# Attention values of a hybrid encoder: one stage for all heads, tokens stationary and weights moving

## The chip, the core and the metric

The kernel runs on one core of a Trainium2 chip. The time is the device time of one launch in microseconds (us) (the span in the profile is the part of it from the first to the last recorded instruction); lower is better. Engines are named TensorE (PE in the profile, PEld for its weight loads), VectorE (DVE), ScalarE (ACT), GpSimd (POOL) and SyncE (SP, which here issues DMAs).

## What is computed

One layer of a streaming encoder for 512 prompt tokens and 64 tokens of a later chunk that share the weights. A combined projection is split among three head groups (a gated delta rule, differential attention, pooling), whose outputs are mixed, and a feed-forward part follows. The change is about `bv`, the values of the attention:

```python
h = rmsnorm(x, norm_mix)                       # (512 + 64) x 1024
proj = jnp.einsum('bld,de->ble', h, w_in)
aq, ak, av, az, aa, ab, bq, bk, bv, cx = split_cols(proj, IN_WIDTHS)
...                                            # A: gated delta rule over aq, ak, av, gate az
bv4 = bv.reshape(bsz, length, B_HEADS, B_DV)   # 4 heads of 128
w = diff_softmax_weights(s, lam)               # softmax_1 - lam * softmax_2
o_b = jnp.einsum('bhqk,bkhe->bqhe', w, bv4)    # later chunk: with 512 cached keys and values ahead
new_v = bv4                                    # an output: p_v, s_v
...                                            # C: pooling over cx
x = x + jnp.einsum('ble,ed->bld', jnp.concatenate([o_a, o_b, o_c], -1), w_out)
x = x + conv_ffn(rmsnorm(x, norm_ffn), ...)
```

## The kernel before

**Tiling.** All 576 tokens stay in SBUF with the features on the partitions. A gemm makes 128 output features for all tokens: the weight tile is stationary, 576 tokens move past it in two parts of 256 and 320 columns (`PARTS`). Each operand is split into a rounded fp32r part and the fp32r remainder (`w_hi` by a ScalarE cast, line 174; `w_lo` by a VectorE subtraction, line 175), and a product is hi x hi + hi x lo + lo x hi. So one gemm (`gemm`, matmuls recorded at line 85) is 8 k tiles x 3 products x 2 parts = 48 matmuls into one accumulator of two PSUM banks (`psg`, named `g`; two such tiles rotate). Four more PSUM banks (`psm`, named `m`) serve everything small.

**Order.** TensorE's instructions are issued in the order in which the program writes them. `projections` is the main stream; it yields after each matmul group, and `drive` then lets the generators that are due (`spawn`) write their own steps in between, by a clock that counts an estimate of TensorE time. A generator that waits for a flag (`after`) makes the stream skip ahead to the next due one, so that no gemm stands between.

**Stages.** `projections` makes, head by head, k, q and v of the delta rule, each followed by a `front(h)` (transposes at line 89, squares, scaling evictions at line 630, then five score matmuls `m<-kq` with a VectorE product at line 643 behind each). When the last front is written, `invert` and `delta_chain` start: the triangular inverse on VectorE, `levels` (small block products, X copies at line 738) and the scan over chunks. Meanwhile the main stream makes four gate gemms, four pooling gemms, and `attn_proj(h)` for each attention head.

**The values before.** `attn_proj(h)` makes three gemms per head; the third is the values, evicted by a ScalarE copy (line 908) into `vT` with features on the partitions. `attention` needs them with tokens on the partitions: `value_rows` transposes five chunks (line 89, `m<-cst,vT`) into two PSUM banks, scales each token's row by `r5` on VectorE (lines 924 and 926, into `v_out`), stores `p_v` and `s_v` by DMA from there, and `attention` goes on after 920 ns of the clock. In the attention, `p` (line 1000) are the softmax weights of a prompt block, `pr` (line 951) those of the later chunk, and `oatt` (line 1031) the scaled output.

**Weights.** `weight_sources` lists the tiles of [128 x 8 x 128] in the order of use; one is fetched and split ahead of use by `weights`.

Of the kernel before, what the change touches and what calls it, by code (L numbers as in the profile page):

```python
# [9 lines left out]
F32 = mybir.dt.float32  # L10
# [5 lines left out]
P = 128  # L16
# [43 lines left out]
def hybrid_step(ctx: ExitStack, tc: tile.TileContext, I, O):  # L60
# [75 lines left out]
    def weight_sources():  # L136
        for h in range(HEADS):
            for t in (4 + h, h, 8 + h):
                yield w_in[t]
        for base in (12, 28):  # L140
            for h in range(HEADS):
                yield w_in[base + h]
        for h in range(HEADS):
            for base in (20, 16, 24):
                yield w_in[base + h]
        for m in range(KT):
            yield w_out[m, :, :8]
        for m in range(2, KT):
            yield w_out[m, :, 8:]
        for f in range(FT):  # L150
            for t in (f, FT + f):
                yield I["ffn_up"][t]
        for m in range(KT - 1):
            for a, b in ((0, 8), (8, 16), (16, FT)):
                yield I["ffn_down"][m, :, a:b]
# [14 lines left out]
    def split_weight(raw):  # L170
        kt = raw.shape[1]
        hi = wp.tile([P, 8, P], F32R, name="w_hi")
        lo = wp.tile([P, 8, P], F32R, name="w_lo")
        nc.scalar.copy(hi[:, :kt], raw)  # L174
        last_split[0] = nc.vector.tensor_sub(lo[:, :kt], raw, hi[:, :kt].bitcast(F32)).ins  # L175
        return [(hi[:, k], lo[:, k]) for k in range(kt)]

    def load_weight():
        if left[0]:
            left[0] -= 1  # L180
            loaded.append(split_weight(pending.pop() if pending else fetch_weight()))
            if left[0] > 4:
                pending.append(fetch_weight())

    def weights():

        if not loaded:
            load_weight()
        ws = loaded.pop(0)
        load_weight()  # L190
        return ws

# [340 lines left out]
    with ExitStack() as ctx2:  # L533
# [6 lines left out]
        def v_tile():  # L540
            return dp.tile([P, TP], F32, name="vT", bufs=3)
# [47 lines left out]
        dq = None  # L589

        starts = (0, P, 2 * P, 3 * P, SO)

        def front(h):
# [56 lines left out]
            if h == HEADS - 1:  # L650
                spawn(invert(), 0)
                spawn(delta_chain(), 0)
# [36 lines left out]
        def levels(pair, inv):  # L689
# [5 lines left out]
            for j, f in enumerate(pair):  # L695
                Xc = f["Xc"] = dq.tile([P, 5, 32], F32, name="Xc", bufs=2)
                XTc = dq.tile([P, 5, 32], F32, name="XTc")
# [12 lines left out]
            for f in pair:  # L710
                U, Xc = f["K"], f["Xc"]
                pa = bank()
                for c in range(5):
                    mm(pa[hi, c * 32:c * 32 + 32], U[lo, c, hi], Xc[lo, c])
                for c in range(4):
                    mm(pa[hi2, c * 32:c * 32 + 32], U[lo2, c, hi2], Xc[lo2, c])
                Y = f["Y"] = dq.tile([P, 5, 32], F32, name="Y", bufs=2)
                nc.scalar.copy(Y[hi], pa[hi, :160].rearrange("p (c x) -> p c x", c=5))
                nc.vector.tensor_copy(Y[hi2, :4], pa[hi2, :128].rearrange("p (c x) -> p c x", c=4))
# [27 lines left out]
        def scan(c):  # L747
# [14 lines left out]
            for f in heads:  # L762
# [3 lines left out]
                else:  # L766
                    mm(f["pa"][:n, 0:P], kq[f["h"]][:, 0, starts[c]:starts[c] + n], f["S"])
                    f["R"] = dq.tile([P, P], F32, name="R", bufs=4)
# [3 lines left out]
            for f in heads:  # L772
                mm(f["pa"][:n, P:2 * P], f["T"][:n, c, :n], f["R"][:n])
                f["e"] = dq.tile([P, P], F32, name="e", bufs=4)
                nc.scalar.copy(f["e"][:n], f["pa"][:n, P:2 * P])
# [117 lines left out]
        def attn_proj(h):  # L893
# [5 lines left out]
            for i in range(3):  # L899
                if i == 2:  # L900
                    if h == 3:
                        yield from after("values0")
                    dst.append(v_tile())
# [6 lines left out]

        astack = ExitStack()

        def attention():
# [3 lines left out]

            def value_rows(srcT, h):
                pp, p5 = bank(), bank()
                for c in range(5):  # L920
                    n = P if c < 4 else NS
                    transpose(pp[:, c * P:(c + 1) * P] if c < 4 else p5[:NS, :P], srcT[:, c * P:c * P + n], ident)
                sb = ap.tile([P, 5, P], F32, name="v_out", bufs=3)
                nc.vector.tensor_mul(sb[:, :4], pp.rearrange("p (c d) -> p c d", c=4),
                                     r5[:, :4].unsqueeze(2).broadcast_to([P, 4, P]))
                nc.vector.tensor_scalar_mul(sb[:NS, 4], p5[:NS, :P], r5[:NS, 4:5])
                nc.sync.dma_start(O["p_v"][h], sb[:, :4])
                nc.sync.dma_start(O["s_v"][h], sb[:NS, 4])
                return sb
# [116 lines left out]
            for h in range(HEADS):  # L1046
                yield from until(lambda: h in aq)
                ckT, cv = nxt
                kT, qT, vf = aq[h]
# [3 lines left out]
                v = value_rows(vf, h)  # L1053
                done.add(f"values{h}")
                yield 920
# [26 lines left out]
        def projections():  # L1082
# [21 lines left out]
            for h in range(HEADS):  # L1104
# [4 lines left out]
                if h == 1:  # L1109
                    nc.sync.dma_start(O["conv"], cout)  # L1110
            for g in range(4):
# [223 lines left out]
def _feeds(inputs):  # L1335
# [4 lines left out]
    def tiles(w):  # L1340
# [9 lines left out]
        "w_in": tiles(np.concatenate([w_in[:, :2048], w_in[:, 2056:]], 1)),  # L1350
        "w_ab": w_in[:, 2048:2056].reshape(KT, P, 8).transpose(1, 0, 2),
# [45 lines left out]
```

## Time and profile before

| | before |
|---|---|
| median of 3 runs | 851.94 us (851.86 to 852.04) |
| profiled execution | 851.25 us |
| its span | 849.5 us |
| TensorE busy | 829.3 us (98%) |
| TensorE weight loads | 804.4 us (95%) |
| VectorE busy | 535.6 us (63%) |
| ScalarE busy | 358.7 us (42%) |
| GpSimd busy | 107.3 us (13%) |

The rows further down come from the profiled execution. Times there are in us from the start of the span unless marked ns. A row of the timeline is a run of like instructions: its start, the time from there to the end of the last of them, the engine, the source line, the operation with output and input tiles, and how many there are. Matmuls are pipelined, so the busy time of a run reaches past the start of the next; the time of issue is the difference between two starts. In brackets stands the idle time before it and what ended that.

### The profile page before, as it was taken

Reading aid. Unit: us, or ns where it says so; the run is one execution under the profiler, and the core shown is the slowest. Engines: PE = TensorE matmul, PEld = TensorE weight load, DVE = VectorE, ACT = ScalarE, POOL = GpSimd, SP = SyncE. Lnnn points to the kernel's source line nnn. Section 1 sums busy time; section 2 is a strip of 40 time slices with the busy share of each in tenths; the row PEclk is TensorE's granted clock in tenths of the full one; section 3 lists DMA queues with packets and bytes.
Section 4 is the critical chain, followed back from the end, with each engine's and each line's share of the span. In section 5 each row is a group of like instructions: output and inputs, shape, how many; then the busy total and the mean of one; then the engine's idle time right before and its main releaser. Section 6 shows DMA issues by size and latency. Waiting matters only on the chain.

```text
span 849.5 us, 15951 instructions
## 1 busy us (share of the span) xinstructions
PE 829.3 (98%) x6350; PEld 804.4 (95%) x6350; DVE 535.6 (63%) x1199; ACT 358.7 (42%) x796; POOL 107.3 (13%) x166
## 2 busy tenths in 40 slices
PE   9989999999999999999999999999999999999996
PEld 9979999999999877789999999999999999999996
DVE  6698867891348667765767677777776773223422
ACT  7366662162444644553543443444433432222322
POOL 2132211210002000000011121121121210000001
PEclk9999999999999999999999999999999999999999
DMA  6242123242204323226622222222222223333313
GB/s 247 76 125 80 57 77 97 98 114 86 76 30 143 109 79 120 95 79 224 229 75 91 85 75 99 76 75 99 76 83 92 75 77 104 97 93 91 118 58 112
DMA packets 39032, 84.83 MB, mean 100 GB/s; under 512 B 9386, under 2 KB 14526, under 8 KB 38958
## 3 DMA queue, kind: packets, MB, share of 16 engines
q1 hardware_dynamic: 37870, 82.31, 29.9%
q10 hardware_dynamic: 1088, 1.51, 0.5%
q8 instruction: 50, 0.82, 0.4%
q14 instruction: 24, 0.20, 0.1%
HBM read 72.98 MB, written 10.82 MB: 99 GB/s over the span
## 4 chain that ended last, share of the span: by engine, by line
PE 89%; DVE 4%; ACT 2%; DMA 2%; issue 1%; ACTq 0%; POOLq 0%; DVEq 0%
PE g L85 76%; PE m L85 11%; PE m L89 3%; DMA w_raw<-in_ffn_down_dram 1%; ACT w_hi L174 1%; DVE w_lo L175 1%; DMA w_raw<-in_w_in_dram 1%; DVE tmp L874 0%; DVE kq L580 0%; DMA w_raw<-in_w_out_dram 0%; DVE oatt L1031 0%; DVE kq L585 0%; DVE p L1000 0%; DVE tmp L562 0%; ACT p L994 0%
## 5 line engine op out<-in xcount | busy, mean ns | idle before, releaser
L85 PE MATMUL g<-wide,w_hi 128*128 128x256 f32 x1472 | 264.7, 300 | 0.4 <-DVE wide L364 0.3
L85 PE MATMUL g<-t,w_hi 128*128 128x256 f32 (+1 forms) x1408 | 242.8, 294 | 0.0
L85 PEld LDWEIGHTS g<-wide,w_hi 128*128 128x128 f32 x1472 | 222.1, 189 | 2.3 <-DVE wide L364 0.6
L85 PEld LDWEIGHTS g<-t,w_hi 128*128 128x128 f32 x1408 | 210.2, 188 | 0.0
L174 ACT CAST w_hi<-w_raw 128x1024 fp32r<-128x1024 f32 (+2 forms) x109 | 110.6, 1015 | 175.8 <-PE g L85 166.5
L85 PE MATMUL g<-wide,w_lo 128*128 128x256 f32 x736 | 160.8, 300 | 0.1
L175 DVE TENSOR_TENSOR w_lo<-w_raw,w_hi 128x1024 fp32r<-128x1024 f32 (+2 forms) x109 | 128.2, 1176 | 49.0 <-ACT w_hi L174 47.9
L85 PE MATMUL g<-t,w_lo 128*128 128x256 f32 x704 | 150.3, 295 | 0.0
L85 PEld LDWEIGHTS g<-wide,w_lo 128*128 128x128 f32 x736 | 123.5, 190 | 2.1 <-issue 1.1
L85 PEld LDWEIGHTS g<-t,w_lo 128*128 128x128 f32 x704 | 117.4, 188 | 0.1
L1256 DVE SCALAR_TENSOR_TENSOR c<-u,par,c 128x511 f32<-128x511 f32 (+3 forms) x176 | 78.9, 510 | 2.5 <-ACT c L1252 2.5
L1259 POOL COPY fout<-u 128x4 f32<-128x4 f32 x44 | 50.9, 1157 | 223.4 <-DVE u L1250 223.4
L1250 DVE TENSOR_TENSOR u<-g,rstd 128x576 f32<-128x576 f32 x44 | 33.3, 758 | 60.0 <-PE g L85 58.4
L85 PE MATMUL g<-w,w_hi 128*128 128x256 f32 (+1 forms) x280 | 48.4, 295 | 0.0
L85 PEld LDWEIGHTS g<-w,w_hi 128*128 128x128 f32 x280 | 42.0, 188 | 0.0
L1252 ACT ACTIVATE c<-u,par 128x576 f32<-128x576 f32 x44 | 38.3, 871 | 4.5 <-DVE u L1250 1.4
L1276 ACT ACTIVATE s<-c 128x576 f32<-128x576 f32 x22 | 15.1, 687 | 45.8 <-DVE c L1258 45.8
L267 POOL TENSOR_TENSOR osc<-sso,mhalf 128x5 f32<-128x5 f32 x8 | 9.4, 1181 | 182.8 <-DVE sso L1026 77.9
L85 PE MATMUL g<-w,w_lo 128*128 128x256 f32 (+1 forms) x140 | 29.9, 295 | 0.0
L1187 ACT ACTIVATE junk<-m 128x128 f32<-128x128 f32 (+1 forms) x40 | 10.8, 273 | 43.5 <-PE m L89 35.2
L1188 DVE TENSOR_TENSOR t<-m,nf 128x128 f32<-128x128 f32 (+1 forms) x40 | 11.2, 289 | 23.5 <-ACT junk L1187 23.5
L85 PE MATMUL g<-kq,w_hi 128*128 128x256 f32 (+1 forms) x128 | 25.1, 305 | 0.0
(317 smaller groups left out, 1016.6 us busy)
## 6 DMA issues: line engine op xcount, KB each, us to landing
w_raw<-in_ffn_up_dram SPq DMA_DIRECT2D x44, 512.0 KB, 3.2
w_raw<-in_w_in_dram SPq DMA_DIRECT2D x30, 512.0 KB, 3.3
w_raw<-in_ffn_down_dram SPq DMA_DIRECT2D x16, 512.0 KB, 3.5
w_raw<-in_w_out_dram SPq DMA_DIRECT2D x8, 512.0 KB, 3.8
w_raw<-in_ffn_down_dram SPq DMA_DIRECT2D x8, 384.0 KB, 3.2
xr<-in_xT_dram SPq DMA_DIRECT2D x8, 288.0 KB, 3.2
x_d<-xr SPq DMA_DIRECT2D x8, 288.0 KB, 2.1
w<-x_d SPq DMA_DIRECT2D x8, 288.0 KB, 5.2
```

The costliest lines, as they stand in the source:

```text
L85: ordered(nc.tensor.matmul(out, lhsT=lhsT, rhs=rhs, start=start, stop=stop), n / 2.4 if rhs.dtype == F32R else max(54, n / 0.6))
L89: ordered(nc.tensor.transpose(out=out, in_=in_, identity=identity), 107)
L174: nc.scalar.copy(hi[:, :kt], raw)
L175: last_split[0] = nc.vector.tensor_sub(lo[:, :kt], raw, hi[:, :kt].bitcast(F32)).ins
L267: nc.gpsimd.tensor_tensor(out, x, epst[:x.shape[0], :x.shape[1]], op=ALU.pow)
L1187: nc.scalar.activation(junk[:n], src, AF.Square, scale=D ** -0.5, accum_out=op["part"][:n, c, m:m + 1])
L1188: nc.vector.tensor_mul(op["yt"][c][m // 4][:n, (m % 4) * P:(m % 4 + 1) * P], src, op["nf"][:n, m * P:(m + 1) * P])
L1250: nc.vector.tensor_mul(u, ps[:, O0:O1], rstd)
L1252: nc.scalar.activation(c, u, AF.Identity, scale=fw[:, 2, t:t + 1], bias=col("ffn_conv_b", t))
L1256: nc.vector.scalar_tensor_tensor(c[:, a + d:b], u[:, a:b - d], fw[:, j, t:t + 1], c[:, a + d:b], op0=ALU.mult, op1=ALU.add)
L1259: nc.gpsimd.tensor_copy(fout[:, :, :, t], u[:, NP - 64:].rearrange("p (s c) -> p s c", c=64)[:, :, 62:])
L1276: nc.scalar.activation(s, cv[0], AF.Silu)
```

## The change

A new stage `attn_values` makes the values of all four heads, with tokens on the partitions from the start. It runs in `projections` behind the second gate gemm and waits until the four fronts are written. For each of four new weight tiles `w_v` (2 k tiles x 512 columns, the four heads beside each other) and each token chunk of 128 (the fifth has 64), a [128 x 128] piece of the tokens is the stationary operand and 512 weight columns move. The accumulators are both `g` tiles, two chunks in each, and one `m` bank for the fifth chunk. At the last weight tile each finished chunk is evicted by four ScalarE activations, which scale by `r5` and write one head's part each.

The third gemm of `attn_proj`, its eviction, `value_rows` and the pause of 920 go; `p_v` and `s_v` are stored straight from the new tiles. The order of the weight tiles follows, and the small tiles of the delta part share one ring of eight buffers.

```diff
 def weight_sources():
...
-        for base in (12, 28):
-            for h in range(HEADS):
-                yield w_in[base + h]
+        for t in (12, 13):
+            yield w_in[t]
+        for j in range(4):
+            yield I["w_v"][j]
+        for t in (14, 15, 28, 29, 30, 31):
+            yield w_in[t]
         for h in range(HEADS):
-            for base in (20, 16, 24):
+            for base in (20, 16):
                 yield w_in[base + h]
...
         def v_tile():
-            return dp.tile([P, TP], F32, name="vT", bufs=3)
+            return dp.tile([P, TP], F32, name="vT", bufs=4)
...
+        def small():
+            return dq.tile([P, 160], F32, name="sm", bufs=8)
...
             if h == HEADS - 1:
+                done.add("fronts")
                 spawn(invert(), 0)
                 spawn(delta_chain(), 0)
...
-                Xc = f["Xc"] = dq.tile([P, 5, 32], F32, name="Xc", bufs=2)
-                XTc = dq.tile([P, 5, 32], F32, name="XTc")
+                Xc = f["Xc"] = small().rearrange("p (c x) -> p c x", c=5)
+                XTc = small().rearrange("p (c x) -> p c x", c=5)
...
-            for i in range(3):
-                if i == 2:
-                    if h == 3:
-                        yield from after("values0")
-                    dst.append(v_tile())
+            for i in range(2):
                 ps = yield from gemm(hmix)
...
+        av = []
+
+        def attn_values():
+
+            yield from after("fronts")
+            pa, pb, p5 = psg.tile([P, 1024], F32, name="g"), psg.tile([P, 1024], F32, name="g"), bank()
+            where = {0: pa[:, :512], 1: pa[:, 512:], 4: p5[:NS], 2: pb[:, :512], 3: pb[:, 512:]}
+            av.extend(v_tile()[:, :5 * P].rearrange("p (c d) -> p c d", c=5) for _ in range(HEADS))
+            for j in range(4):
+                weights()
+                hi, lo = this[0]
+                for c, ps in where.items():
+                    n = P if c < 4 else NS
+                    for k in range(2):
+                        xh, xl = (x[:, c * P:c * P + n] for x in hmix[2 * j + k])
+                        wh, wl = (w[:, 4 * k:4 * k + 4].rearrange("p h d -> p (h d)") for w in (hi, lo))
+                        for i, (x, w) in enumerate(((xh, wh), (xh, wl), (xl, wh))):
+                            mm(ps, x, w, start=j + k + i == 0, stop=j == 3 and k == 1 and i == 2)
+                            yield False
+                    if j == 3:
+                        for h in range(HEADS):
+                            nc.scalar.activation(av[h][:n, c], ps[:, h * P:(h + 1) * P], AF.Copy, scale=r5[:n, c:c + 1])
...
-            def value_rows(srcT, h):
-                pp, p5 = bank(), bank()
-                for c in range(5):
-                    n = P if c < 4 else NS
-                    transpose(pp[:, c * P:(c + 1) * P] if c < 4 else p5[:NS, :P], srcT[:, c * P:c * P + n], ident)
-                sb = ap.tile([P, 5, P], F32, name="v_out", bufs=3)
-                nc.vector.tensor_mul(sb[:, :4], pp.rearrange("p (c d) -> p c d", c=4),
-                                     r5[:, :4].unsqueeze(2).broadcast_to([P, 4, P]))
-                nc.vector.tensor_scalar_mul(sb[:NS, 4], p5[:NS, :P], r5[:NS, 4:5])
-                nc.sync.dma_start(O["p_v"][h], sb[:, :4])
-                nc.sync.dma_start(O["s_v"][h], sb[:NS, 4])
-                return sb
...
-                v = value_rows(vf, h)
-                done.add(f"values{h}")
-                yield 920
+                nc.sync.dma_start(O["p_v"][h], v[:, :4])
+                nc.sync.dma_start(O["s_v"][h], v[:NS, 4])
...
                 if h == 1:
                     nc.sync.dma_start(O["conv"], cout)
+                    yield from attn_values()
...
+        "w_v": w_in[:, 3080:3592].reshape(4, 2, P, 512).transpose(0, 2, 1, 3).reshape(4, P, 8, P),
```

Three places in the order of the instructions. Each row is the line, the operation, output and input tiles, the shape, and the engines or queues whose semaphores the instruction waits for (`x3` is three like it in a row).

TensorE, the scores of the last delta front (`m<-kq`), before: six gemm matmuls of the third gate gemm (`g<-wide`) stand between one score and the next.

```order
L85 MATMUL g<-wide,w_lo 128x256
L85 MATMUL g<-wide,w_lo 128x320
L85 MATMUL m<-kq 128x256
L85 MATMUL g<-wide,w_hi 128x256 [waits PE_49]
L85 MATMUL g<-wide,w_hi 128x320
L85 MATMUL g<-wide,w_hi 128x256
L85 MATMUL g<-wide,w_hi 128x320
L85 MATMUL g<-wide,w_lo 128x256 [waits DVE_49]
L85 MATMUL g<-wide,w_lo 128x320
L85 MATMUL m<-kq 128x256 [waits Activation_49]
```

TensorE, the same place after:

```order
L85 MATMUL g<-wide,w_lo 128x256
L85 MATMUL g<-wide,w_lo 128x320
L85 MATMUL m<-kq 128x256
L85 MATMUL m<-kq 128x256 [waits Activation_49] x3
L85 MATMUL m<-kq 128x128 [waits DVE_49]
L85 MATMUL g<-w_hi,wide 128x512 [waits PE_49]
L85 MATMUL g<-w_lo,wide 128x512
```

The five scores now stand in a row, with the waits of the second to the fifth behind each other, and the new stage (`g<-w_hi,wide`, 512 columns) follows.

TensorE, the last weight tile of the new stage, from the second half of chunk 0 over chunk 1 to chunk 4 (`m<-`):

```order
L85 MATMUL g<-w_hi,wide 128x512 x2
L85 MATMUL g<-w_lo,wide 128x512
L85 MATMUL g<-w_hi,wide 128x512
L85 MATMUL g<-w_hi,wide 128x512 [waits Activation_49]
L85 MATMUL g<-w_lo,wide 128x512
L85 MATMUL g<-w_hi,wide 128x512 x2
L85 MATMUL g<-w_lo,wide 128x512
L85 MATMUL g<-w_hi,wide 128x512
L85 MATMUL m<-w_hi,wide 64x512
```

The first matmul of chunk 1 waits for ScalarE; by its semaphore's value that is for the fourth of the evictions of chunk 0. The first matmul of chunk 3 has the same wait for those of chunk 2.

ScalarE, the X copies of the first pair of levels (`X<-m`, line 738), before, with a weight's cast and the eviction of a value gemm (`vT<-g`) ahead of them:

```order
L706 COPY XT<-XTc 32x5x32 [waits DVE_49,Pool_49]
L706 COPY XT<-XTc 32x5x32 x3
L174 CAST w_hi<-w_raw 128x1024 [waits DMAHW5_49,PE_49,Activation_49]
L908 COPY vT<-g 128x576 [waits PE_49]
L738 COPY X_2161<-m 64x256 [waits PE_49]
L738 COPY X_2175<-m 64x256 [waits PE_49]
L691 ACTIVATE XT<-m 64x4x64 [waits PE_49] x2
```

ScalarE, the same copies after (line 753 there), with the copies into XT ahead of them:

```order
L721 COPY XT<-sm 32x5x32 [waits DVE_49,Pool_49]
L721 COPY XT<-sm 32x5x32 x3
L753 COPY X_2002<-m 64x256 [waits PE_49]
L753 COPY X_2016<-m 64x256 [waits PE_49]
L706 ACTIVATE XT<-m 64x4x64 [waits PE_49] x2
```

The cast and the eviction no longer stand between the XT copies and the X copies.

## Rows read from the trace of the kernel before

**Rows 1.** page, parts 1 and 2: TensorE's busy time, granted clock by slice.

```profile
PE 829.3 (98%) x6350; PEld 804.4 (95%) x6350; DVE 535.6 (63%) x1199; ACT 358.7 (42%) x796; POOL 107.3 (13%) x166
...
PEclk9999999999999999999999999999999999999999
```

**Rows 2.** waits of TensorE: line, released by: us, times, longest.

```profile
PE m L89 <- DVE p L1000: 3.0, 4, 1.0
...
PE m L89 <- ACT pr L951: 1.9, 2, 0.9
```

**Rows 3.** chain of waits, feed-forward part: start us, length us, what.

```profile
717.72 17.51 PE g L85 x132
```

**Rows 4.** timeline of TensorE, 826 to 837: start, busy, line, tiles, form.

```profile
826.85 1.92 PE L85 MATMUL m<-wide,u 128*128 128x320 f32 x12
828.61 4.56 PE L85 MATMUL m<-w,t 128*128 128x320 f32 x30
...
834.75 1.56 PE L85 MATMUL m<-wide,c 128*128 128x256 f32 x12
836.15 1.56 PE L85 MATMUL m<-wide,u 128*128 128x256 f32 x12
```

**Rows 5.** timeline of TensorE, 300 us: sample scores, 512 columns.

```profile
300.16 1.08 PE L85 MATMUL m<-ckT,kq 64*64 64x512 f32 x4
301.07 0.29 PE L85 MATMUL m<-kq 64*64 64x64 f32 x4
```

**Rows 6.** timeline of TensorE, 272 and 326 us: value transposes and what follows.

```profile
272.29 0.71 PE L89 MATMUL m<-cst,vT 128*128 128x128 f32 x5
272.75 0.51 PE L85 MATMUL g<-wide,w_hi 128*128 128x256 f32 x2
...
326.03 0.71 PE L89 MATMUL m<-cst,vT 128*128 128x128 f32 x5
...
326.60 0.51 PE L85 MATMUL g<-wide,w_lo 128*128 128x256 f32 x2
```

**Rows 7.** timeline of TensorE, 123 to 129 us: scores of the last delta front.

```profile
123.85 0.59 PE L85 MATMUL m<-kq 128*128 128x256 f32 x2
124.10 0.89 PE L85 MATMUL g<-wide,w_hi 128*128 128x256 f32 x4
...
128.93 0.78 PE L85 MATMUL g<-wide,w_hi 128*128 128x256 f32 x4
```

**Rows 8.** timeline of ScalarE, 121 to 126 us: that front's evictions.

```profile
122.26 1.15 ACT L630 ACTIVATE kt<-m,wt 128x128 f32<-128x128 f32 x4 [0.93 <-DVE wt L625]
123.28 0.65 ACT L630 ACTIVATE vs<-m,root 128x128 f32<-128x128 f32 x2
...
124.03 0.93 ACT L630 ACTIVATE vs<-m,root 128x128 f32<-128x128 f32 x3
```

**Rows 9.** timeline of ScalarE, 188 us: a value gemm's eviction, the X copies.

```profile
188.53 0.64 ACT L908 COPY vT<-g 128x576 f32<-128x576 f32 x1
189.19 0.64 ACT L738 COPY X<-m 64x256 f32<-64x256 f32 x2
```

**Rows 10.** timeline of TensorE, 189 us: the level behind these copies.

```profile
189.62 1.14 PE L85 MATMUL m<-XT,X 64*64 64x64 f32 x16 [0.87 <-ACT X L738]
```

**Rows 11.** timeline of ScalarE, 332 us: sample softmax in the attention.

```profile
332.12 0.78 ACT L951 ACTIVATE pr<-m,mx,qscale 128x512 f32<-128x512 f32 x1 [1.05 <-DVE mx L949]
```

**Rows 12.** timeline of TensorE, 333 us: transposes of the attention's output.

```profile
333.04 0.66 PE L89 MATMUL m<-cst,oatt 128*128 128x128 f32 x4 [0.94 <-ACT pr L951]
```

**Rows 13.** windows: length, busy PE, PEld, DVE, ACT, POOL; clock, DMA share.

```profile
300.00:320.00 20.00, 19.34 (x132) 15.20 (x132) 14.20 (x47) 10.59 (x28) 1.17 (x1) 1.00 0.26 84
...
360.00:380.00 20.00, 18.32 (x137) 16.05 (x136) 13.95 (x51) 11.06 (x34) 0.00 (x0) 1.00 0.28 84
```

**Rows 14.** instructions by line: count, ns min/median/max, first, last start.

```profile
L924 DVE TENSOR_TENSOR v_out<-m,r x4: 683/691/691, 273.9 to 353.4; 128x512 f32<-128x512 f32 x4
...
L926 DVE TENSOR_SCALAR v_out<-m,r x4: 332/333/335, 274.5 to 354.0; 64x128 f32<-64x128 f32 x4
```

More of the change, by code (lines that the diff above doesn't have):

```diff
@@ L175, in split_weight @@
         last_split[0] = nc.vector.tensor_sub(lo[:, :kt], raw, hi[:, :kt].bitcast(F32)).ins
+        whole[0] = hi, lo
         return [(hi[:, k], lo[:, k]) for k in range(kt)]
+    whole = [None]
+    wholes = []
     def load_weight():
@@ L181, in load_weight @@
             loaded.append(split_weight(pending.pop() if pending else fetch_weight()))
+            wholes.append(whole[0])
             if left[0] > 4:
@@ L189, in weights @@
         ws = loaded.pop(0)
+        this[0] = wholes.pop(0)
         load_weight()
         return ws
+    this = [None]
     def gemm(xs):
@@ L716, in levels @@
                     mm(pa[hi2, c * 32:c * 32 + 32], U[lo2, c, hi2], Xc[lo2, c])
-                Y = f["Y"] = dq.tile([P, 5, 32], F32, name="Y", bufs=2)
+                Y = f["Y"] = small().rearrange("p (c x) -> p c x", c=5)
                 nc.scalar.copy(Y[hi], pa[hi, :160].rearrange("p (c x) -> p c x", c=5))
@@ L767, in scan @@
                     mm(f["pa"][:n, 0:P], kq[f["h"]][:, 0, starts[c]:starts[c] + n], f["S"])
-                    f["R"] = dq.tile([P, P], F32, name="R", bufs=4)
+                    f["R"] = small()[:, :P]
                     nc.vector.scalar_tensor_tensor(f["R"][:n], f["pa"][:n, 0:P], ngam[:n, c, f["h"]:f["h"] + 1],
@@ L773, in scan @@
                 mm(f["pa"][:n, P:2 * P], f["T"][:n, c, :n], f["R"][:n])
-                f["e"] = dq.tile([P, P], F32, name="e", bufs=4)
+                f["e"] = small()[:, :P]
                 nc.scalar.copy(f["e"][:n], f["pa"][:n, P:2 * P])
@@ L1048, in attention @@
                 ckT, cv = nxt
-                kT, qT, vf = aq[h]
+                (kT, qT), v = aq[h], av[h]
                 nc.sync.dma_start(O["k"][h], kT[:, :T])
```

## The prediction

> **What bounds the kernel now.** I read the page first. TensorE is busy for 829.3 us, 98% of a span of 849.5, and its granted clock stands at 9 tenths or more in all 40 slices, the 2.4 GHz level [rows 1]. So there is no idle stage in which a change can hide: what shortens TensorE's own stream shortens the kernel, and a new wait on TensorE lengthens it, unless it takes the place of an old one. Second, the chain of waits: a stretch of gemm is one unbroken piece, 132 matmuls in 17.51 us, which is 132.7 ns each for a mix of 256 and 320 columns [rows 3]. Third, the list of what TensorE waits for: the waits that this change can touch are 3.0 us for the softmax weights `p` from VectorE and 1.9 us for `pr` from ScalarE [rows 2], both in the attention, and one wait of 0.87 us for ScalarE's X copy in the delta part [rows 9, 10]. Last, the timeline around each place that the change edits, and the windows of 20 us over the attention: TensorE is idle 0.66 us in 300 to 320 and 1.68 in 360 to 380 [rows 13]; the two windows between are like the last, so the four leave about 5.6 us.
>
> **The change, part by part.**
>
> *Columns (T1).* Before, a value gemm of one head is 48 matmuls (8 k tiles, 3 products, parts of 256 and 320 columns), so four heads are 192 x 132.7 ns = 25.5 us. After, one stage has 4 weight tiles x 5 token chunks x 2 k tiles x 3 products = 120 matmuls of 512 columns. The fifth chunk is 64 tokens, which are now the stationary side, so it streams 512 columns like a full one: 120 x 512 = 61,440 columns against 96 x 576 = 55,296. What does a column cost? Away from the gemms, 12 matmuls of 320 columns are issued in 828.61 - 826.85 = 1.76 us, 146.7 ns each, and 12 of 256 in 836.15 - 834.75 = 1.40, 116.7 each [rows 4]. Both are 0.456 to 0.458 ns a column, with no fixed part, so 512 would be 234.7. The nearest row of that very width, four of 512 columns and half the contraction, is issued in 301.07 - 300.16 = 0.91 us, 227.5 each [rows 5]. I take the middle, 231: 27.7 us, hence +2.2 us. The ends are 512 columns at the full 2.4 GHz, 213.3 ns (+0.1), and 234.7 (+2.7).
>
> The Trainium skill, "TensorE: Matmul & The Clock Gate", section "Back-to-back issue gap", gives for an isolated warm matmul N / 2.4 + 2.5 ns, and for a stream of weight loads and matmuls about 131 ns at 512 columns. By the first T1 would be 25.9 - 25.5 = +0.4, by the second 15.7 - 25.5 = -9.8. The rows speak against both: the first would make 256 and 320 columns 109.2 and 135.8, and the second would have a column of a wide matmul cost half of what it does here.
>
> *The waits at the last weight tile (T2).* After the last products of a chunk, four ScalarE activations scale its rows into the four heads' tiles. The order shows that at the last weight tile the first matmul of chunk 1 and of chunk 3 wait for ScalarE, for all four evictions of chunks 0 and 2: two chunks share one accumulator tile, and the wait is for the tile, though they lie in different halves of it. Nothing stands between to cover it, since matmuls are issued in order and the delta work is not due there. One such wait: the tail of the chunk's last matmul, 0.17 (the four of 512 columns take 1.08 busy and 0.91 to the next issue [rows 5]), about 0.1 until ScalarE starts, the four activations 1.15 (four of 128 columns from PSUM [rows 8]), and 0.14 for the release (ScalarE's `pr` ends at 332.12 + 0.78 = 332.90 and TensorE starts at 333.04 [rows 11, 12]). That is 1.56, less what the queued weight load saves; I take 1.5, twice: +3.0. Ends: 1.1 each if only the activations count, 123.28 - 122.26 = 1.02 from the first of four to the next behind them [rows 8], and 1.7 each if the release takes its 0.14 both into ScalarE and out of it and nothing overlaps: 2.2 to 3.4. Chunk 4 lies in a bank of its own, and the next gemm takes a free tile, so there is no third wait.
>
> *The value transposes (T3).* Twenty fp32 transposes leave TensorE, five a head. Five are issued in 272.75 - 272.29 = 0.46 us; in the second place 326.60 - 326.03 = 0.57 holds five and one transpose of `p` more, 0.47 for five [rows 6]. Four times 0.47 is -1.9. Ends: -1.4 if one of the four stood in a wait and saved nothing, -2.8 if each saves its busy 0.71.
>
> *The scores of the last front (T4).* The stage waits for all four delta fronts, because it takes both gemm accumulators at once. The last front's five score matmuls, which stood between groups of six gemm matmuls, are now five in a row, and no gemm covers what they wait for. Before, from the first score at 123.85 to the gemm matmul behind the fifth at 128.93 there are 5.08 us, of which 24 gemm matmuls at 132.7 ns are 3.18: 1.9 for the five [rows 7]. After, the second to fourth wait for ScalarE, whose evictions of that front end at 124.03 + 0.93 = 124.96 [rows 8], and the fifth for VectorE's first decay product, which reads the first scores and gives back their bank; I put its end 0.3 to 0.5 behind ScalarE's, an estimate from the length of one operation on a tile of this size. From 123.85 that is 1.5 to 1.6. So -0.35; ends -0.8 (the clump costs no more than its own issue, four of 124.10 - 123.85 = 0.25 and a short one, 1.1) and +0.9 (VectorE has another operation ahead of it, as long as ScalarE's 0.93).
>
> *The levels (T5).* Before, ScalarE evicts a head's value gemm for 0.64 us directly ahead of the X copies, and TensorE waits 0.87 for these [rows 9, 10]. After, no such eviction and no cast stands there in ScalarE's order. -0.6; ends 0 (VectorE or the bank comes next) and -0.9.
>
> *The attention (T6).* VectorE loses the two scaling evictions, 0.69 + 0.33 us a head, 4.1 in all [rows 14], and the pause of 920 ns behind them goes too. That pause is the point: the scores come earlier by the time that VectorE is given back, so its queue at the next `p` is as long as before. The transposes of one head start at 326.03 [rows 6], and the stall that follows six microseconds later is VectorE, then ScalarE's `pr`, then TensorE at 333.04 [rows 11, 12], a chain that none of these evictions is in. By hand along VectorE's order the three stalls after the change come to about what they are now: 0. Ends: -3.0 (the `p` waits vanish, as they are VectorE's) and +1.9 (each `pr` wait doubles) [rows 2].
>
> *At nothing.* The count of weight loads is the same, and the split of a tile still has one tile's products, 30 x 0.231 = 6.9 us, to hide in; if that cover were gone it would cost a cast per tile. The delta inversion keeps its VectorE time. The value rows' DMAs are the same bytes. The small delta tiles share one ring of 8 buffers, and no row of TensorE's order got a wait from it.
>
> *Sum.* +2.2 + 3.0 - 1.9 - 0.35 - 0.6 + 0 = +2.35 us. The profiled execution took 851.25, so 853.6 by its own measure; it lies 0.69 under the median of 851.94, to which the same +2.35 gives **854.3 us**.
>
> **The rivals.**
>
> *Full rate.* Long matmuls of 512 columns run at 213.3 ns, since the extra that 256 and 320 show is paid by changing weights often. For it: half as many weight loads a column. Against it: 227.5 at 512 [rows 5]. T1 falls by 2.1: 852.2.
>
> *VectorE relieved.* The `p` and `pr` waits go with the 4.1 us that VectorE no longer spends: 854.3 - 4.9 = 849.4, faster. For it: the largest wait is VectorE's [rows 2]. Against it: the pause that goes with them.
>
> *The attention jams.* Scores that start 0.92 us earlier for every head meet VectorE still at the scaling of the previous head's output, and the `pr` stall doubles: 854.3 + 1.9 = 856.2, further on the slow side. It decides once the head's first scores wait for more than VectorE's scaling.
>
> *Savings at their ends.* T3 at -2.8, T4 at -0.8, T5 at -0.9 make 0.9 + 0.45 + 0.3 = 1.65 less: 852.6, no difference.
>
> *Wide matmuls stream two columns a cycle.* At the page's 131 ns the stage is 15.7 us instead of 27.7: 854.3 - 12.0 = 842.3, faster. The mechanism would be a fixed part in each matmul, and rows 4 leave none.
>
> The change doing nothing at all is no rival here: the order has the transposes gone and the 512-column rows in.
>
> **How the numbers follow.** About 0.2% (1.7 us) is what a measurement of this kernel can tell from no change, so slower begins at 853.6 and faster ends at 850.2. My forecast has 0.45, and with the terms about 0.8 us to either side 0.31 of that lies above 853.6 and 0.14 below. Full rate 0.13 (no difference), VectorE relieved 0.17 (faster), attention jams 0.13 (slower), savings at their ends 0.10 (no difference), two columns a cycle 0.02 (faster). Slower 0.44, same 0.37, faster 0.19. The range runs from the relieved VectorE's 849.4 to the jam's 856.2 with the forecast's 0.8 on top, 857.0; the forecast's own is 853.5 to 855.1.
>
> **What would show it.** T1: the mean time between issues of the 512-column rows, 227 to 235. T2: two waits of TensorE for ScalarE's value tiles, about 1.3 us idle each. T3: no transposes of the value tiles. T4: a wait of about 0.5 for ScalarE or VectorE at the last scores. T5: no wait for the X copy. T6: in the four windows of the attention, idle time near 5.6. The prediction is wrong if the 512-column rows take under 220 ns, if the waits of the last tile are missing, or if the attention's idle time moves by over 2 us.

## The result, and the profile after

The changed kernel takes 863.05 us (median of four, 861.87 to 864.26) against 851.99 for the kernel before beside it: a ratio of 1.0126, 95% interval 1.0114 to 1.0138. That is 11 us slower where 2.35 were forecast, and above the range. The profiled execution took 862.72, its span is 860.9 (before 849.5). The first two parts of its page, the rows that answer to [rows 1]:

```profile
PE 833.9 (97%) x6258; PEld 799.9 (93%) x6258; DVE 534.0 (62%) x1191; ACT 363.8 (42%) x812; POOL 103.9 (12%) x166
...
PEclk9999999999999999999999999999999999999999
```

A slice of the clock's row is 21.5 us long, so a stretch of 3.41 us at half clock still reads 9 there; the windows further down show one. TensorE is busy 4.6 us longer, and idle for 6.8 us more. The list of what it waits for, which answers to [rows 2], shows where the idle time is (line numbers are those of the changed kernel):

```profile
PE g L85 <- ACT vT L943: 2.5, 2, 1.2
PE m L89 <- DVE stat L1012: 2.4, 1, 2.4
PE g L85 <- DVE w L1258: 1.6, 1, 1.6
PE m L85 <- DVE U L814: 1.6, 1, 1.6
PE m L89 <- ACT pr L972: 1.5, 1, 1.5
...
PE g L85 <- DVE wide L1154: 1.0, 2, 0.5
PE m L85 <- ACT sm L790: 0.7, 1, 0.7
```

Two of these were in the sum: the value tiles (L943, term T2) and `pr`. The wait for X, 0.87 [rows 10], is off the list, and so by name is the one for `p`, 3.0 us before. New are a wait put down to the softmax statistics (L1012), one for `U` in the scan (L814), one for `w` at the start of the second half of the output projection (L1258), and those for the pooling rows' conversion (`wide`, L1153 and L1154: ScalarE and VectorE make the two parts of an operand of the output projection out of an accumulator tile).

The stage itself is as costed. TensorE's timeline, from the last front's scores to the gemm behind the stage:

```profile
123.98 2.27 PE L85 MATMUL m<-kq 128*128 128x256 f32 x10
126.00 0.48 PE L85 MATMUL g<-w_hi,wide 128*128 128x512 f32 x1
...
147.71 0.39 PE L85 MATMUL g<-w_hi,wide 128*128 128x512 f32 x1
149.33 0.50 PE L85 MATMUL g<-w_hi,wide 128*128 128x512 f32 x1 [1.24 <-ACT vT L943]
...
154.97 0.50 PE L85 MATMUL g<-w_hi,wide 128*128 128x512 f32 x1 [1.24 <-ACT vT L943]
...
156.47 0.69 PE L85 MATMUL g<-wide,w_hi 128*128 128x256 f32 x4
```

The stage runs from 126.00 to 156.47, 30.47 us. Each of the two waits costs 149.33 - 147.71 = 1.62 where 0.23 is usual, so 1.4; without them there are 27.7 us for 120 matmuls, 230.6 ns each. The 1.62 is the last matmul's busy 0.39, 0.03 to ScalarE's start at 148.13, 1.15 for its four activations, and 0.05 to TensorE's. The five scores take 126.00 - 123.98 = 2.02.

In the scan, VectorE's timeline and TensorE's wait:

```profile
243.55 0.76 DVE L917 TENSOR_TENSOR kq<-g,rstd 128x576 f32<-128x576 f32 x1 [0.18 <-PE g L85]
244.36 1.23 DVE L178 TENSOR_TENSOR w_lo<-w_raw,w_hi 128x1024 fp32r<-128x1024 f32 x1
...
246.28 0.28 DVE L814 TENSOR_TENSOR U<-tq,m 128x128 f32<-128x128 f32 x1
```

```profile
246.62 0.49 PE L85 MATMUL m<-S,kq 128*128 128x128 f32 x2 [1.64 <-DVE U L814]
```

The end of a gemm (its eviction `kq`, then the split `w_lo` of the next weight) now stands in VectorE's order ahead of the scan's own operations, the last of which here is the addition to `U` that the next small matmul needs: 0.76 + 1.23 us in a chain with no room for them.

In the attention the same happens, and more behind it. TensorE, then VectorE, then the windows of 2 us (columns as in [rows 13]):

```profile
365.33 0.70 PE L85 MATMUL m<-a 64*128 64x256 f32 x4
368.46 0.59 PE L89 MATMUL m<-cst,p 128*128 128x128 f32 x3 [2.43 <-DVE stat L1012]
```

```profile
364.91 0.76 DVE L1164 TENSOR_TENSOR xr<-xr,g 128x576 f32<-128x576 f32 x1
365.58 1.22 DVE L178 TENSOR_TENSOR w_lo<-w_raw,w_hi 128x1024 fp32r<-128x1024 f32 x1
...
367.04 0.75 DVE L1011 TENSOR_REDUCE stat<-m 128x1 f32<-128x256 f32 x2
367.70 0.61 DVE L1021 SCALAR_TENSOR_TENSOR p<-p,stat,p 128x384 f32<-128x384 f32 x1
368.23 0.22 DVE L1012 TENSOR_SCALAR stat<-stat,qneg 128x2 f32<-128x2 f32 x1
```

```profile
366.00:368.00 2.00, 0.03 (x2) 0.00 (x0) 2.00 (x8) 0.00 (x0) 0.00 (x0) 1.00 0.53 164
368.00:370.00 2.00, 1.54 (x8) 1.57 (x9) 0.84 (x5) 1.51 (x5) 0.00 (x0) 0.69 0.71 192
370.00:372.00 2.00, 2.00 (x12) 1.99 (x10) 1.23 (x3) 0.59 (x2) 0.00 (x0) 0.50 0.21 78
372.00:374.00 2.00, 2.00 (x16) 1.83 (x16) 0.29 (x1) 0.41 (x2) 0.00 (x0) 0.95 0.78 217
```

TensorE issues scores at 365.33 and comes to the transposes of `p`. By the program's semaphores they wait for the `p` of line 1021, which ends at 367.70 + 0.61 = 368.31; the profile names the statistics, which end closest to the start. VectorE did not come to `p` earlier because the end of a gemm of the output projection (`xr`, 0.76) and of a weight (`w_lo`, 1.22) and then the next block's reductions stood ahead of it. So it is a wait for `p` as before, but of 2.43 us, where the longest was 1.0 [rows 2]. Straight behind that its granted clock is at 0.50, the 1.2 GHz level, until about 372; the clock's record has it there for 3.41 us, worth up to 1.7 us of matmuls. The profile of before has no such stretch ahead of its last few us.

Last, the chain of waits at the change from the attention's memory to that of the feed-forward part:

```profile
400.73 0.32 SPq L170
...
401.10 5.25 DMA w<-x_d
...
406.44 0.77 DVE w L1258
```

VectorE's first `w` waits for the read of `x_d`, which is issued behind a weight's load and takes 5.25 us, and TensorE waits 1.65 us for that `w`. The chain of before has no such read, though the kernel issues it at the same place: there it landed after 3.65 us, in time. The wait is about as long as the read was longer.

### The profile page after: what moved, and what is told of

Same layout as the page of the kernel before. It is cut to its first block, busy times and chain, and to the rows that moved or that the text cites. A ratio compares the mean times of both kernels' runs of the same rounds, so it can differ in the third digit from the quotient of the medians.

```text
span 860.9 us, 15758 instructions
## 1 busy us (share of the span) xinstructions
PE 833.9 (97%) x6258; PEld 799.9 (93%) x6258; DVE 534.0 (62%) x1191; ACT 363.8 (42%) x812; POOL 103.9 (12%) x166
## 4 chain that ended last, share of the span: by engine, by line
PE 88%; DVE 5%; DMA 3%; ACT 2%; issue 1%; POOL 0%; ACTq 0%; POOLq 0%; SPq 0%; DVEq 0%
PE g L85 74%; PE m L85 11%; PE m L89 2%; DMA w_raw<-in_ffn_down_dram 1%; DVE w_lo L178 1%; DVE stat L1011 1%; DMA w<-x_d 1%; ACT w_hi L177 1%; DMA w_raw<-in_w_in_dram 1%; ACT p L1015 1%; DVE kq L591 0%; ACT vT L943 0%; DVE p L1021 0%; DVE oatt L1052 0%; DVE kq L596 0%
## 5 line engine op out<-in xcount | busy, mean ns | idle before, releaser
L85 PE MATMUL g<-wide,w_hi 128*128 128x256 f32 x1344 | 242.3, 300 | 2.7 <-DVE w L1258 1.6
L85 PEld LDWEIGHTS g<-wide,w_hi 128*128 128x128 f32 x1344 | 202.9, 189 | 5.8 <-issue 2.8
L85 PE MATMUL g<-wide,w_lo 128*128 128x256 f32 (+1 forms) x672 | 147.2, 301 | 0.4 <-DVE w_lo L178 0.4
L85 PEld LDWEIGHTS g<-wide,w_lo 128*128 128x128 f32 x672 | 112.7, 190 | 2.3 <-issue 1.1
L1015 ACT ACTIVATE p<-m,stat,qscale 128x512 f32<-128x512 f32 (+3 forms) x32 | 19.5, 614 | 14.9 <-DVE stat L1012 14.8
```

Source lines behind the costliest of these rows:

```text
L85: ordered(nc.tensor.matmul(out, lhsT=lhsT, rhs=rhs, start=start, stop=stop), n / 2.4 if rhs.dtype == F32R else max(54, n / 0.6))
L1015: nc.scalar.activation(p_m[:, :nk], maps[m], AF.Exp, scale=qscale[:, j:j + 1], bias=st[:, m:m + 1], accum_out=st[:, 2 + m:3 + m])
```

## The experiments

All are compared with the kernel before, run beside them (medians of 851.9 to 852.6).

**The distance of the heads.** The planner's clock puts the attention's heads 23.6 to 24.5 us apart before and 21.9 after: the pause of 920 ns and five transposes of 107 ns had held them apart. e1_pace puts that back:

```diff
                 nc.sync.dma_start(O["s_v"][h], v[:NS, 4])
+                yield 1455
```

> The changed kernel with one line more: a pause of 1455 ns of the planner's clock where the value transposes (5 x 107) and the 920 ns stood, so that the attention's heads are again about 24 us of that clock apart instead of 21.9. Theory (packing: heads planned closer than VectorE and ScalarE can serve them): the 2.4 us wait for the softmax statistics and the 1.5 us wait for pr shrink, the stretch at 1.2 GHz behind the long wait goes, the wait of 1.6 us at the start of the second half of the output projection goes: 863.05 - about 5 = 857.5 to 859. Rival (phase of the main stream's gemms, not the packing): the waits move to other places, 861.5 to 864.

It took 859.62 us, 3.4 below the changed kernel, two thirds of what the theory gave and between the two ranges. The wait of 2.43 and the one for `w` are gone, and no stretch at 1.2 GHz lies behind the delta part; three waits for `p` (2.3 in all) and two for the conversion (1.3 and 0.8) are there. Such comparisons have some chance in them: this profiled execution has two stretches of 3.41 us at 1.2 GHz, 30 and 53 us after the start, where the instructions are still those of the changed kernel, whose profile has none there. It comes to the scan's wait for `U` 1.47 us later for that (248.09 against 246.62).

e3_before_packed does the reverse in the kernel before:

```diff
+                then = clock[0]
                 v = value_rows(vf, h)
+                clock[0] = then
                 done.add(f"values{h}")
-                yield 920
```

> The kernel before with its value gemms and transposes, but the transposes uncounted on the planner's clock and the pause of 920 ns left out, so that its attention heads are about 21.8 us of that clock apart, as in the changed kernel. Theory (packing): its attention stalls grow as they did in the change, by 2 to 5 us, 854 to 857, perhaps with a stretch at 1.2 GHz. Rival (packing is harmless, the main stream's phase decides): 851 to 853.

It took 854.8, ratio 1.0026 (1.0009 to 1.0044), 2.2 more than before, with the very wait of the change in it (TensorE's timeline):

```profile
343.52 0.52 PE L89 MATMUL m<-cst,p 128*128 128x128 f32 x3 [2.43 <-DVE stat L991]
```

So a shift of the planner's clock alone makes that wait, with no part of the new stage in the program. A longer pause in the changed kernel, 2900 ns, was to show a trend:

> The changed kernel with a pause of 2900 ns of the planner's clock per attention head and nothing else, so that the heads are 25.1 us apart. Theory (packing): not above e1_pace, 857 to 859.5, the two waits of 1.24 us at the last weight tile still there. Rival (at 24 us the packing is undone, and what is left is the place of the main stream's steps): a longer pause changes the waits without a trend, 859 to 862.

It took 858.0, as the theory had it. But a longer pause in the kernel before, `yield 2400` for `yield 920`, did the opposite:

> The kernel before with its pause at 2400 ns instead of 920, heads 25.2 us of the clock apart instead of 23.6. Theory (the stalls of the attention come from heads too close): the waits for p and pr, 4.9 us, fall to 2 to 3 and the time to 849 to 851. Rival (the kernel before sits where the places of the steps happen to fit, and any shift is for the worse): 852.5 to 855.

It took 858.8, ratio 1.0068 (1.0046 to 1.0090): 6.2 us slower by a pause alone, against the theory and beyond the rival's range. ScalarE's timeline, TensorE's, and the windows show why:

```profile
283.52 0.77 ACT L994 ACTIVATE p<-m,stat,qscale 128x512 f32<-128x512 f32 x1
...
284.27 1.04 ACT L174 CAST w_hi<-w_raw 128x1024 fp32r<-128x1024 f32 x1
285.21 0.64 ACT L908 COPY vT<-g 128x576 f32<-128x576 f32 x1
```

```profile
282.48 1.20 PE L85 MATMUL g<-xp,tmp 128*128 128x256 f32 x6
285.90 0.79 PE L85 MATMUL g<-kq,w_hi 128*128 128x256 f32 x4 [2.23 <-ACT vT L908]
```

```profile
284.00:286.00 2.00, 0.10 (x1) 0.10 (x1) 1.52 (x4) 2.00 (x5) 0.00 (x0) 1.00 0.00 0
...
288.00:290.00 2.00, 2.00 (x8) 1.21 (x8) 0.00 (x0) 0.47 (x2) 0.00 (x0) 0.50 0.67 229
290.00:292.00 2.00, 2.00 (x10) 1.31 (x7) 1.09 (x4) 0.16 (x1) 0.00 (x0) 0.50 0.04 8
292.00:294.00 2.00, 2.00 (x10) 1.72 (x9) 0.63 (x4) 1.84 (x5) 0.00 (x0) 0.50 0.00 0
```

A value gemm's eviction (L908) had come to stand in ScalarE's order behind two exponentials of a softmax and a cast. TensorE needed that accumulator at about 283.7 and got it at 285.90, and the clock went to the 1.2 GHz level for 6.83 us. Packing as a law falls: not the distance counts, but what the ends of the gemms meet in the queues of ScalarE and VectorE.

**The two waits at the last weight tile.** e2_chunks takes the chunks in another order:

```diff
-where = {0: pa[:, :512], 1: pa[:, 512:], 4: p5[:NS], 2: pb[:, :512], 3: pb[:, 512:]}
+where = {0: pa[:, :512], 2: pb[:, :512], 4: p5[:NS], 1: pa[:, 512:], 3: pb[:, 512:]}
```

> The changed kernel with the token chunks in the order 0, 2, 4, 1, 3 instead of 0, 1, 4, 2, 3, so that the two chunks of one accumulator tile do not follow each other and their evictions lie under other chunks. Theory (term T2 is a plain cost): both waits of 1.24 us vanish and 2.5 to 2.8 us with them, 860.3 to 860.6, the rest of the trace as it was. Rival (everything behind is shifted and the stalls behind take it back or add to it): the waits vanish too, but the total moves by something else than 2.5, 858 to 863.

It took 860.0, 3.0 less, just outside the theory's range and within the rival's. Both waits are gone. The stage itself shows what that is worth (TensorE's timeline, its first row and the gemm behind it):

```profile
125.91 0.48 PE L85 MATMUL g<-w_hi,wide 128*128 128x512 f32 x1
...
153.33 0.80 PE L85 MATMUL g<-wide,w_hi 128*128 128x256 f32 x4
```

It takes 27.42 us instead of 30.47, so T2 is a plain cost of 3.05, the size forecast. The waits put down to the statistics (2.4) and to `U` (1.6) stay, at the same steps 3 to 5 us earlier, but the trace behind is not as it was, as the rival had it: the one for `w` is gone. The profiled execution, the fastest of ten (856.73 to 862.02), has a span 5.9 shorter, so the 3.0 between the medians is not T2 by itself. The Trainium skill, "PSUM — Partial Sum Buffer", section "PSUM bank collisions raise a hardware error", wants two engines kept apart by bank; chunks 0 and 1 lie in different banks, so by that rule TensorE need not have waited for ScalarE. It was the program's wait for the whole tile that cost this.

**Both**, e4_both:

> Both edits of the changed kernel, the pause of 1455 ns and the chunk order 0, 2, 4, 1, 3. Theory (packing and the two waits are separate costs that add): 863.05 - 5 - 2.6 = about 855.5, 854.5 to 856.5; what is left over the kernel before is the columns and the delta part. Rival (phase): anywhere within 856 to 862.

It took 859.18: not the sum; 3.4 and 3.0 alone, 3.9 together. Here the conversion of the pooling rows comes late (ScalarE, TensorE, windows):

```profile
307.41 0.77 ACT L1015 ACTIVATE p<-m,stat,qscale 128x512 f32<-128x512 f32 x1
...
308.16 0.73 ACT L1154 ACTIVATE wide<-g,par 128x576 fp32r<-128x576 f32 x1
```

```profile
308.95 0.53 PE L85 MATMUL g<-wide,w_hi 128*128 128x256 f32 x2 [1.28 <-ACT wide L1154]
310.29 0.53 PE L85 MATMUL g<-wide,w_hi 128*128 128x256 f32 x2 [0.81 <-DVE wide L1155]
```

```profile
312.00:314.00 2.00, 2.00 (x10) 1.49 (x9) 1.16 (x1) 0.47 (x2) 0.00 (x0) 0.50 0.39 147
314.00:316.00 2.00, 2.00 (x7) 0.92 (x8) 0.37 (x2) 0.00 (x0) 0.00 (x0) 0.50 0.82 276
```

ScalarE's part (L1154 there) stands behind the second exponential. TensorE waits 1.28 and 0.81 us, and 6.83 us at the lower level follow. The two waits are not what is missing from the sum, for e1_pace has them as well, with no stretch behind them:

```profile
312.42 0.53 PE L85 MATMUL g<-wide,w_hi 128*128 128x256 f32 x2 [1.28 <-ACT wide L1154]
313.76 0.54 PE L85 MATMUL g<-wide,w_hi 128*128 128x256 f32 x2 [0.81 <-DVE wide L1155]
323.43 0.52 PE L89 MATMUL m<-cst,p 128*128 128x128 f32 x3 [0.96 <-DVE wide L1061]
```

The last of these rows is at 322.99 in e4_both. Up to the first wait e4_both is 312.42 - 308.95 = 3.47 us ahead of e1_pace, at the third 323.43 - 322.99 = 0.44: 3.03 us of that lead were lost over the stretch at 1.2 GHz between them.

**Where the conversions and the stage stand.** e5_start starts the attention later (`yield 3000` to `yield 9000` at its head), e8_later moves the stage behind the third gate gemm (`if h == 2:`, and the weights' order with it), e6_delta starts the levels 1500 ns later (`yield 2300` to `yield 3800`); all on top of e4_both.

> The changed kernel with the pause and the chunk order of e4_both, and the attention started 6000 ns of the planner's clock later, so that the pooling rows are converted (ScalarE and VectorE, from the accumulator tile) 4.6 us after the attention's first scores instead of 16.6; in the kernel before it is 6.5. Theory (the conversions wait in ScalarE's and VectorE's order behind the softmax of the next head): the two waits for them, 1.3 and 0.8 us, go, and with them the stretch at 1.2 GHz behind: 859.2 - 2.1 - about 2 = 854.5 to 856. Rival (each shift brings another collision): the waits for the conversions go and others of the same size come, 858 to 861.

It took 856.38, between theory and rival. The waits for the conversions are nearly gone (0.3 left), and one of 2.4 put down to the statistics is back, with 3.41 us at the lower level behind it.

> The changed kernel with the pause and the chunk order of e4_both, and the stage of the values behind the third gate gemm instead of the second, when the last front is written and nothing has to be waited for; the scores of the last front lie between gemm matmuls again. By term T4 this alone saves nothing that can be seen: the clump of scores took 2.02 us against 1.9. Theory (the phase of the main stream decides the rest): the total moves by more than that, either way, 855 to 861, by waits in the scan and the attention that change. Rival (the place of the stage costs by itself): 858.5 to 859.5 with the same waits as e4_both.

It took 857.08, as the theory had it. The wait for `U` is gone, and the attention's waits are others (four of 4.3 in all put down to `m`, a bank that VectorE clears; one of 2.0 for `p`).

> The changed kernel with the pause and the chunk order of e4_both, and the delta levels and scan started 1500 ns of the planner's clock later, so that the ends of the gemms (an eviction of 0.76 us and a split of 1.23 us on VectorE, a cast of 1.05 on ScalarE) fall elsewhere in the scan. Theory (the wait of 1.6 us for U in the scan is one of phase): it goes or falls under 0.5, and 859.2 becomes about 857.8. Rival (it comes from the shared ring of small tiles, which leaves the scan less room): the wait stays at 1.6, 859.2.

It took 859.91. The wait for `U` falls to 0.7, so it was one of place, and the attention behind has new ones. Whether the later start won anything by itself is not shown: the four runs lie between 856.0 and 860.83, and the profiled execution has 10.24 us at 1.2 GHz within its first 60 us, where its instructions are those of e4_both, and is 2.88 us behind it by then (55.44 against 52.56 at the same wait).

**One part alone that is harmless**, the ring of small tiles in the kernel before:

> The kernel before with one part of the change alone: the small tiles of the delta part in one ring of eight buffers. Theory (phase): no wait for U, the time that of the kernel before within 0.7. Rival (the ring): the wait of about 1.6 us for U shows here too, 853.5 to 855.

It took 852.62, ratio 0.9997 (0.9984 to 1.0010), with no wait for `U`: the ring alone makes no difference clear of noise.

**Variations on e8_later**: the attention 3000 or 6000 ns later, a longer pause, and a late start without the pause.

> As e8_later (stage behind the third gate gemm, chunk order 0, 2, 4, 1, 3, pause of 1455 ns), and the attention started 3000 ns of the planner's clock later, so that the pooling rows are converted 5.3 us behind its first scores, as in the kernel before (6.5). Theory (packing and the place of the conversions make what is left): the waits of the attention fall to about those of before, 4.9 us, and the time to 852.5 to 854.5. Rival (each shift meets new collisions): 856 to 858, as e8_later.

> As e9_start6 with 6000 ns later instead of 3000, so that the conversions stand 0.5 us behind the first scores. Theory: 852.5 to 855, a little worse than e9_start6 if the attention's end now comes so late that the last gemms of the output projection have nothing beside them. Rival: 856 to 859.

> As e8_later with the pause at 2900 ns of the planner's clock instead of 1455, so that the attention's heads are 25.1 us apart instead of 24. Theory (packing): the waits in the attention fall further, 853 to 855.5. Rival (24 us is enough, other collisions remain): 856 to 858.

> As e10_start9 without the pause: the attention starts as late, and its heads are 21.9 us of the clock apart, as in the changed kernel. Theory (packing costs by itself, wherever the stage and the conversions stand): 2 to 4 us over e10_start9. Rival (packing mattered only through the place of the conversions): within 1 us of e10_start9.

They took 858.91, 855.78, 854.89 and 857.10. The first lies above what theory and rival gave, with waits of 2.0 and 1.9 us and two stretches at 1.2 GHz, and its five runs spread from 855.94 to 863.26; the pause is worth 1.3 us between the second and the last, less than was expected. e11_pace2 is the best form with the new stage, ratio 1.0033 (1.0017 to 1.0048), 2.9 us over before: its profiled execution, the fastest of five, has a span of 851.2, 1.7 over before, and no stretch at the lower level ahead of the last few us.

**A version that beats both.** With the ring there is room for a fourth value tile in the kernel before, and the last head need not wait for the first:

```diff
-            return dp.tile([P, TP], F32, name="vT", bufs=3)
+            return dp.tile([P, TP], F32, name="vT", bufs=4)
...
-                    if h == 3:
-                        yield from after("values0")
```

> The kernel before with the ring of e7_ring and a fourth tile for the values, so that the last head's value gemm waits for no earlier head; the planner's clock then ends 2.8 us earlier and everything behind the delta part shifts by up to that. Theory (places of the steps): a shift changes the waits by one or two us either way, 850 to 854, with the conversions at other places behind the softmax. Rival (only the heads' distance counts, which is as before): within 0.7 of the kernel before.

It took 849.72, ratio 0.9968 (0.9952 to 0.9985), 2.9 less than before. The sums over 300 to 380 us (length, TensorE's busy time, then the others) of before, of the changed kernel and of this one:

```profile
sum 80.00, PE 74.45 PEld 61.99 DVE 57.08 ACT 41.73 POOL 3.50; mean PE 18.61 PEld 15.50 DVE 14.27 ACT 10.43 POOL 0.87
```

```profile
sum 80.00, PE 73.18 PEld 59.90 DVE 54.31 ACT 41.34 POOL 3.50; mean PE 18.30 PEld 14.97 DVE 13.58 ACT 10.34 POOL 0.88
```

```profile
sum 80.00, PE 77.66 PEld 65.09 DVE 57.83 ACT 42.40 POOL 3.50; mean PE 19.42 PEld 16.27 DVE 14.46 ACT 10.60 POOL 0.87
```

TensorE is idle 5.6, 6.8 and 2.3 us there. The heads stand about as far apart as before on the planner's clock; what shifted are the conversions and the ends of the gemms against them.

## Why the prediction was wrong

**Right: T1, T2 and the stage.** T1 gave 231 ns a matmul and +2.2; measured are 230.6 and 27.7 - 25.5 = +2.2. The rival of the full rate (213.3) and that of two columns a cycle (131) fall with it. The Trainium skill's figure of about 131 ns for a stream of 512 columns ("TensorE: Matmul & The Clock Gate", section "Back-to-back issue gap") does not hold here: the trace has 230.6. T2 gave +3.0; the profile shows 2 x 1.4 = 2.8, and taking it away made the stage 3.05 shorter. Two of its pieces were a little too large: 0.1 until ScalarE starts, for which it had no row (0.03 measured), and 0.14 for the release (0.05). What it put at nothing, an unchanged count of weight loads, holds for the tiles fetched; TensorE's own loads fell from 6350 to 6258 in the pages. T3: the transposes of the value tiles are out of the attention; its -1.9 was not measured by itself.

**T4, small.** The clump cost 2.02 against 1.9, not 1.5 to 1.6: +0.1 for -0.35.

**T5, incomplete.** The wait for X went, as forecast, and the scan got one of 1.64 instead. The named waits of the delta part went from 0.87 + 0.69 to 0.69 + 1.64, +0.8 instead of -0.6. I followed one wait out of the order and did not look at what the shifted gemms would meet four steps on.

**T6, the step that failed.** The sentence was that the scores come earlier by the time that VectorE is given back, so its queue is as long as before, and the sum 0, between -3.0 and +1.9. It took VectorE's own total for its queue. What stands in that queue is the work at the ends of the main stream's gemms, two or three operations of 0.7 to 1.2 us in a row, and where it falls in a head's chain is set by the planner's clock, which the change shifted throughout: the conversions stood 6.5 us of that clock behind the first scores before, and 19.3 after. Idle time in 300 to 380 grew by 6.82 - 5.55 = 1.27, in 280 to 300 by 0.48. In place of 0 the attention thus cost 1.75 us of idle time, and up to 1.7 more for the slow clock behind its longest wait. The idle part lies within the term's own ends and under the 2 us that the prediction named as a sign: that sign looked at idle time, and the slow clock shows as busy time. The rival of the jam had the right kind of mechanism and the wrong price: it let `pr` double, where one wait for `p` grew to 2.43.

**Not in the sum at all.** The clock: up to +1.7 for 3.41 us at 1.2 GHz behind that wait. The prediction saw a clock that never fell and took it as given. And the wait for the read of `x_d`, +1.65. The read took 5.25 us here and 4.5 in e13_pace_only2 and 4.7 in e8_later, which have such a wait (2.0 and 1.0), but 3.6 to 3.7 before and in e1_pace, e2_chunks and e4_both, which have none. Why it lands late in some profiles, and whether the change has a part in that, stays open.

Together: 2.2 + 2.8 - 1.9 + 0.1 + 0.8 + 1.75 + 1.7 + 1.65 = 9.1 of the 11.4 us between the two spans, with T3's -1.9 as forecast and the clock at its most. The other 2.3 were not ascribed. e14_before_pace and e15_before_noskip, 6.2 slower and 2.9 faster by edits that take no work out and put none in, show that terms of this size come and go in this kernel with the places of its steps. What stays open is a rule that would give the waits without a run: neither the heads' distance nor the conversions' place was one by itself.

## What to carry to other kernels

Where a planner interleaves two streams and the helper engines work in order, an edit that takes time out of one stream shifts every later meeting of the two, and such a shift is not a cost of zero: give it a range of its own, here some 3 us down and 6 up, from trials of the same kernel with a pause longer or shorter. Look in the helper engines' order for the big operations at a gemm's end (eviction, cast, split) and ask which chain they will stand in. An eviction that makes the next group wait for its tile is the plain kind of cost: it can be read off the rows, and an order of the groups that alternates tiles takes it away.

## What the runs showed of the hardware

A wait of about 2 us could be followed by a stretch at the lower level of TensorE's clock. In the attention the stretches at 0.50 are 3.41 us long, twice 6.83. Of the waits of 1.87 us and over in the attention, seven had one within 3 us behind them (2.43 in the changed kernel; 2.44, 2.43, 2.02, 1.96, 1.87 and 2.23 in e2_chunks, e5_start, e6_delta, e9_start6, e12_nopace and e14_before_pace), and five had none (2.43, 2.02, 1.90, 2.43 and 2.02 in e3_before_packed, e8_later, e9_start6, e11_pace2 and e13_pace_only2). In e4_both one followed two shorter waits, 1.28 and 0.81, which stand in e1_pace too with none behind them, and one stretch in e9_start6 has no wait over 1.2 straight ahead of it. So the same wait can be followed by a stretch or not, and no run here shows what decides.

Further stretches lie some 28 and 53 us after the start in several profiles, where all the kernels still run the same instructions: e1_pace has both, e7_ring the first, before and the changed kernel neither. Near 53 us TensorE waits 2.7 us for VectorE, near 28 us it has no wait over 0.3. In e6_delta these two cost 2.88 us, so they alone can put executions of one kernel that far apart.
